# HGRN level scores with a stationary tile cut to the keys that a level uses

## The chip, the cores and the metric

The kernel runs on one core of one Trainium2 chip. The metric is the device time of one execution in microseconds. A profile of one execution, with the start and duration of every instruction on every engine, stands beside the times.

## What is computed

One hybrid decoder layer on 512 tokens of width 1024, in float32: a half-step SwiGLU network, a token mixer, and a second half-step SwiGLU network, each between RMS norms and added to its input. The mixer has four HGRN2 heads and four mLSTM heads, all causal. The change touches the scores of HGRN2:

```python
rel = G[:, :, :, None, :] - G[:, :, None, :, :]       # G: running sum of log forget gates
decay = jnp.exp(jnp.where(causal, rel, -jnp.inf))
scores = jnp.sum(qc[:, :, :, None, :] * kc[:, :, None, :, :] * decay, axis=-1)
o = o_inter + jnp.einsum("bhts,bhsv->bhtv", scores, vc)
```

The decay between a query and a key differs for each of the 128 channels, so that a score is no plain product of q and k.

## The kernel before

**The whole.** Three parts follow one another: the first SwiGLU network, the mixer, the second SwiGLU network. Almost all of TensorE's time goes into their large matrix products, done in split precision: every weight tile is split into a high part (ScalarE, line 273) and a low part (VectorE, line 275) of the format fp32r, and three products stand for one. The mixer's input projections are such products as well; lines 533 and 179 to 181 issue them. The small products of the mixer itself are plain float32.

**How HGRN scores are formed.** The sequence is handled in four chunks of 128 tokens, and the four heads as two pairs (`p` = 0 and 1), so that a pair has 8 blocks of 128 x 128 scores (2 heads x 4 chunks). Within such a block the diagonal is one product (`hgrn_diag`, line 1342). Everything below it is covered by seven levels, `LEVELS = (1, 64, 32, 16, 8, 4, 2)`. A level of size c cuts the 128 tokens into groups of 2c; queries are those in the second half of each group, keys those in the first half, and both are scaled by the decay to the group's middle, which makes the score a plain product. So each level has 64 queries and 64 keys of the 128 tokens. The queries are packed (64 columns, tile `qe`); the keys lie in their places in a tile of 128 columns (`ke`), whose other places hold older values. The product is thus 128 keys x 64 queries, and a mask (`mask`, one per level) picks the entries that count when they are copied to the score tile `sT` (line 1306). The last key that a level of size c uses is token 127 - c. Level 1 is different: one product with a column of ones (line 1298).

**Instructions of one level and pair.** VectorE and ScalarE prepare `qe` and `ke` (lines 1284 to 1291; the Exp of line 1287 writes the keys). TensorE then has 8 products (line 1302), one for each block of scores: the stationary tile is the keys (128 channels x 128 columns), the moving one the 64 queries, and all 8 go into one PSUM bank of 512 columns. VectorE copies under the mask.

**Order.** `hgrn_levels` steps through the levels of a pair by hand, each level being a generator that yields between its stages, so that the vector work of level n+1 is issued ahead of the product of level n. Between the steps `fill(per)` issues pieces of the mixer's input projections (`FILL` gives 6 pieces for the first pair, 5 for the second), which are filler work for TensorE. The two `ke` tiles alternate between levels, so the Exp of level n+2 waits for the product of level n. Each engine works through its own instructions in order. `job_rows` (line 1387) has a stationary tile of 100 columns, and the mLSTM scores (line 1476) use 64 of the 128 rows of the array.

Of the kernel before, what the change touches and what calls it, by code (L numbers as in the profile page):

```python
# [14 lines left out]
P = 128  # L15
# [100 lines left out]
class Layer:  # L116
# [179 lines left out]
    def flat(self, v):  # L296
        return v.rearrange("p a b -> p (a b)")
# [962 lines left out]
    def hgrn_edges(self, p, d):  # L1260
# [4 lines left out]
        for a in range(2):  # L1265
# [2 lines left out]
                nc.tensor.transpose(pt[:, c * P : (c + 1) * P], d[:, a, c * P : (c + 1) * P], self.ident)  # L1268
            nc.scalar.copy(self.kdt[:, 2 * p + a, :], pt[:, : 3 * P])

    def hgrn_level(self, p, n, ke):

        nc = self.nc
        c = LEVELS[n]
        q, kk, G = self.q[p], self.kk[p], self.G[p]
        flat = lambda t: t.rearrange("p a t -> p (a t)")
        blk = lambda t: flat(t).rearrange("p (b two c) -> p b two c", two=2, c=c)
        qe = self.st("qe")
        qe3 = qe.rearrange("p (b c) -> p b c", c=c)
        if c > 1:  # L1280
            el = self.st("el")
            el3 = el.rearrange("p (b c) -> p b c", c=c)
            ref = blk(G)[:, :, 0, c - 1 : c].broadcast_to([P, 512 // c, c])
            nc.vector.tensor_tensor(qe3, blk(G)[:, :, 1, :], ref, op=ALU.subtract)
            nc.vector.tensor_tensor(el3, ref, blk(kk)[:, :, 0, :], op=ALU.subtract)
            nc.scalar.activation(qe, qe, AF.Exp)
            nc.scalar.activation(blk(ke)[:, :, 0, :], el3, AF.Exp)
        else:
            nc.vector.tensor_scalar(qe3, blk(kk)[:, :, 1, :], -1.0, 1.0, op0=ALU.mult, op1=ALU.add)
        yield  # L1290
        nc.vector.tensor_tensor(qe3, qe3, blk(q)[:, :, 1, :], op=ALU.mult)
        if c == 1:

            nc.vector.tensor_tensor(qe3, qe3, blk(kk)[:, :, 0, :], op=ALU.mult)
        yield
        sc = self.ps()
        if c == 1:
            nc.tensor.matmul(sc, self.one.broadcast_to([P, P]), qe, start=True, stop=True)
        else:
            k8, q8 = flat(ke).rearrange("p (n s) -> p n s", s=P), qe.rearrange("p (n u) -> p n u", u=64)  # L1300
            for m in range(8):
                nc.tensor.matmul(sc[:, 64 * m : 64 * m + 64], k8[:, m], q8[:, m], start=True, stop=True)  # L1302
        yield
        so = self.sT[:, 8 * p : 8 * p + 8, :].rearrange("p n (b two c) -> p n b two c", two=2, c=c)[:, :, :, 1, :]
        mk = self.mask[:, n : n + 1, :].broadcast_to([P, 8, 64]).rearrange("p n (b c) -> p n b c", c=c)
        nc.vector.copy_predicated(so, mk, sc.rearrange("p (n b c) -> p n b c", n=8, c=c))
        yield

    def hgrn_levels(self, p, kes, per, then=lambda: None):
# [502 lines left out]
```

## Time and profile before

| | |
|---|---|
| median of 3 runs | 940.24 us (940.08 to 941.1) |
| profiled execution: span from first to last instruction | 938.5 us |
| TensorE clock granted over the span | 0.999 |
| busy share of the span: TensorE, VectorE, ScalarE, GpSimdE | 99%, 82%, 55%, 11% |
| passes of line 1302 | 192, started between 403.3 and 482.7 us |

In the profile's rows PE is TensorE's matmul, PEld its weight load (which runs beside matmuls), DVE is VectorE, ACT ScalarE, POOL GpSimdE; "q" behind an engine is its sequencer. L1302 is line 1302. A row of a group gives line, engine, operation, written and read tiles, shapes and the count; the stationary tile of a matmul stands as rows * columns ahead of the moving tile. Matmuls overlap in the pipeline, and their ends are modelled, so the distance between starts says more than a duration.

### The profile page before, as it was taken

How to read it: one execution, taken by the hardware profiler on the slowest of the kernel's cores; microseconds unless marked ns; L12 is line 12 of the kernel's file. 1: busy time of each engine (PE TensorE's matmuls, PEld its weight loads, DVE VectorE, ACT ScalarE, POOL GpSimd, SP SyncE). 2: the span in 40 equal slices, each digit the busy share in tenths (PEclk: the TensorE clock that was granted, in tenths of full speed). 3: DMA queues.
4: the chain of work that ended last, by engine and by line, in shares of the span. 5: the costliest groups of instructions: out<-in, count | busy, mean ns of one | idle time of the engine just before them, and what ended most of it. 6: DMA issues, size and time to landing. Idle time of an engine off the chain costs nothing.

```text
span 938.5 us, 18056 instructions
## 1 busy us (share of the span) xinstructions
PE 930.2 (99%) x7471; PEld 895.9 (95%) x7471; DVE 772.4 (82%) x1044; ACT 511.9 (55%) x735; POOL 107.4 (11%) x172
## 2 busy tenths in 40 slices
PE   9999999999999999999999999999999999999997
PEld 7999999999999999998887888899999999999997
DVE  6899988889988876698846564799899989998884
ACT  7645555557456467956622444495454545655541
POOL 3530000000001045200001210314000000000101
PEclk9999999999999999999999999999999999999999
DMA  9252433332352024321312124352354434323212
GB/s 319 87 157 91 126 123 113 93 111 72 118 170 90 24 84 124 111 68 45 91 45 68 45 76 139 123 173 65 124 158 135 135 115 156 113 87 121 87 45 90
DMA packets 86956, 101.35 MB, mean 108 GB/s; under 512 B 4277, under 2 KB 66777, under 8 KB 86874
## 3 DMA queue, kind: packets, MB, share of 16 engines
q1 hardware_dynamic: 86586, 99.68, 34.0%
q8 instruction: 58, 0.95, 0.4%
q10 hardware_dynamic: 288, 0.52, 0.2%
q14 instruction: 24, 0.20, 0.1%
HBM read 98.10 MB, written 2.10 MB: 107 GB/s over the span
## 4 chain that ended last, share of the span: by engine, by line
PE 63%; ACT 1%; issue 0%; DVE 0%; DVEq 0%; POOLq 0%; POOL 0%; ACTq 0%
PE ps L603 22%; PE ps L893 7%; PE ps L533 6%; PE ps L901 5%; PE ps L179 5%; PE ps L181 5%; PE ps L180 5%; PE ps L1302 2%; PE ps L543 1%; PE ps L348 1%; PE ps L1476 0%; PE ps L1387 0%; PE ps L1583 0%; PE ps L1556 0%; PE ps L1342 0%; PE ps L1580 0%
## 5 line engine op out<-in xcount | busy, mean ns | idle before, releaser
L273 ACT CAST w<-raw 128x1024 fp32r<-128x1024 f32 (+1 forms) x238 | 244.6, 1035 | 230.3 <-PE ps L603 93.5
L275 DVE TENSOR_TENSOR w<-raw,w 128x1024 fp32r<-128x1024 f32 (+1 forms) x238 | 290.9, 1228 | 36.3 <-ACT w L273 35.8
L603 PE MATMUL ps<-xq,w 128*128 128x256 f32 x2016 | 237.1, 277 | 0.0
L603 PEld LDWEIGHTS ps<-xq,w 128*128 128x128 f32 x2016 | 232.9, 188 | 0.0
L603 PE MATMUL ps<-sq,w 128*128 128x256 f32 x1512 | 177.9, 276 | 0.3
L603 PEld LDWEIGHTS ps<-sq,w 128*128 128x128 f32 x1512 | 174.3, 188 | 0.9 <-ACT ps L654 0.9
L893 PE MATMUL ps<-w,hs 128*128 128x256 f32 x960 | 113.0, 276 | 0.0
L893 PEld LDWEIGHTS ps<-w,hs 128*128 128x128 f32 x960 | 110.7, 188 | 0.0
L289 DVE TENSOR_TENSOR raw<-raw,raw 128x1024 f32<-128x1024 f32 x72 | 89.8, 1251 | 6.1 <-DMA raw<-in_ffn_w_in_dram 4.5
L179 PE MATMUL ps<-w,xq 128*128 128x512 f32 x192 | 78.7, 411 | 0.1
L180 PE MATMUL ps<-w,xq 128*128 128x512 f32 x192 | 74.9, 391 | 0.0
L181 PE MATMUL ps<-w,xq 128*128 128x512 f32 x192 | 74.9, 392 | 0.0
L438 POOL TENSOR_SCALAR col<-col 128x1 f32<-128x1 f32 x24 | 8.9, 372 | 513.7 <-ACT junk L437 513.7
L901 PE MATMUL ps<-w,hs 128*128 128x256 f32 x480 | 57.7, 276 | 0.0
L533 PE MATMUL ps<-xq,w 128*128 128x256 f32 x480 | 56.4, 278 | 0.0
L901 PEld LDWEIGHTS ps<-w,hs 128*128 128x128 f32 x480 | 55.9, 188 | 0.0
L533 PEld LDWEIGHTS ps<-xq,w 128*128 128x128 f32 x480 | 55.2, 188 | 0.5 <-issue 0.5
L179 PEld LDWEIGHTS ps<-w,xq 128*128 128x128 f32 x192 | 36.1, 188 | 8.3 <-issue 0.9
L181 PEld LDWEIGHTS ps<-w,xq 128*128 128x128 f32 x192 | 36.0, 188 | 8.1 <-DVE xq L355 0.3
L812 ACT CAST hs<-hf 128x1024 fp32r<-128x1024 f32 x32 | 33.6, 1052 | 17.6 <-PE ps L901 10.8
L180 PEld LDWEIGHTS ps<-w,xq 128*128 128x128 f32 x192 | 36.2, 188 | 7.0 <-DVE w L281 0.3
L813 DVE TENSOR_TENSOR hs<-hf,hs 128x1024 fp32r<-128x1024 f32 x32 | 39.0, 1219 | 1.3 <-ACT hs L812 1.2
(258 smaller groups left out, 1147.5 us busy)
## 6 DMA issues: line engine op xcount, KB each, us to landing
raw<-in_ffn_w_in_dram SPq DMA_DIRECT2D x98, 512.0 KB, 3.6
raw<-in_ffn_w_out_dram SPq DMA_DIRECT2D x44, 512.0 KB, 3.9
raw<-in_w_mix_in_dram SPq DMA_DIRECT2D x28, 512.0 KB, 3.6
raw<-in_w_mix_out_dram SPq DMA_DIRECT2D x8, 512.0 KB, 3.8
out_dram<-xs SPq DMA_DIRECT2D x8, 256.0 KB, 2.0
xs<-in_x_dram SPq DMA_DIRECT2D x6, 256.0 KB, 4.2
gpost<-in_norm_post_dram SPq DMA_DIRECT2D x3, 512.0 KB, 3.6
gpre<-in_norm_pre_dram SPq DMA_DIRECT2D x2, 512.0 KB, 3.8
```

What stands on the lines that cost most here:

```text
L179: mm(ps, sh, mh, start=start, stop=False, **kw)
L180: mm(ps, sh, ml, start=False, stop=False, **kw)
L181: mm(ps, sl, mh, start=False, stop=stop, **kw)
L273: nc.scalar.copy(hi, raw)
L275: self.low = nc.vector.tensor_tensor(lo, raw, hi.bitcast(F32), op=ALU.subtract)
L289: (nc.vector if late else nc.gpsimd).tensor_tensor(o, o, c, op=ALU.add)
L533: mm(ps[:, u0:u1], w[:, a, k, :], self.xop(k, b, u0, u1), start=k + n + m == 0, stop=k == ND - 1 and n == 2, skip_group_check=True,)
L603: self.nc.tensor.matmul(ps[:, c], wb[b][:, k, v], left[d][:, k, :], start=first and a + n + k == 0, stop=n == 2 and k == KH - 1, skip_grou ...
L812: self.nc.scalar.copy(hi, src)
L813: self.nc.vector.tensor_tensor(lo, src, hi.bitcast(F32), op=ALU.subtract)
L893: mm(out, a[kk][:, i * P : (i + 1) * P], w[:, b, kk, QUARTER * v : QUARTER * (v + 1)], start=begin and c == kk == n == 0, stop=kk == 1 and ...
L901: mm(ps[:, QUARTER * c : QUARTER * (c + 1)], A[a][:, c], B[b], start=begin and c == n == 0, stop=n == 2, skip_group_check=True,)
```

## The change

The stationary tile of a level's 8 products is cut to the first r columns: r = 128 - c, but not less than 72. That is 72, 96, 112, 120, 124 and 126 columns for the levels 64, 32, 16, 8, 4 and 2. The product then writes only the first r partitions of the bank, and the masked copy reads and writes only these. The entries left out are those that every mask had left out. Level 1 keeps 128. Lines behind the new function move down (1302 becomes 1307, 1306 becomes 1312).

```diff
+    def rows(self, c):
+
+        return P if c == 1 else max(P - c, 72)
+
     def hgrn_level(self, p, n, ke):
...
             k8, q8 = flat(ke).rearrange("p (n s) -> p n s", s=P), qe.rearrange("p (n u) -> p n u", u=64)
+            r = self.rows(c)
             for m in range(8):
-                nc.tensor.matmul(sc[:, 64 * m : 64 * m + 64], k8[:, m], q8[:, m], start=True, stop=True)
+                nc.tensor.matmul(sc[:r, 64 * m : 64 * m + 64], k8[:, m, :r], q8[:, m], start=True, stop=True)
         yield
+        r = self.rows(c)
         so = self.sT[:, 8 * p : 8 * p + 8, :].rearrange("p n (b two c) -> p n b two c", two=2, c=c)[:, :, :, 1, :]
         mk = self.mask[:, n : n + 1, :].broadcast_to([P, 8, 64]).rearrange("p n (b c) -> p n b c", c=c)
-        nc.vector.copy_predicated(so, mk, sc.rearrange("p (n b c) -> p n b c", n=8, c=c))
+        nc.vector.copy_predicated(so[:r], mk[:r], sc.rearrange("p (n b c) -> p n b c", n=8, c=c)[:r])
```

## The prediction

> **What bounds the kernel now.** I read the engine rows of the page first, then its chain, then the chain of waits between 400 and 490 us, where all edited instructions lie, and the windows and TensorE's waits behind that stretch.
>
> ```profile
> span 938.5 us, 18056 instructions
> PE 930.2 (99%) x7471; PEld 895.9 (95%) x7471; DVE 772.4 (82%) x1044; ACT 511.9 (55%) x735; POOL 107.4 (11%) x172
> PE 63%; ACT 1%; issue 0%; DVE 0%; DVEq 0%; POOLq 0%; POOL 0%; ACTq 0%
> ```
>
> The row of engines alone does not settle it, because matmul ends are modelled; but nearly everything else on the chain has a share of 0 or 1% and TensorE has 63%. TensorE is an in-order stream of matmul passes from end to end. Now the stretch itself, as columns busy time (count) for each engine, and, in the second fence, the longest waits in front of weight loads from 400 us on (total us, times, longest):
>
> ```profile
> 400.00:490.00 90.00, 90.00 (x595) 81.10 (x594) 68.59 (x100) 45.53 (x62) 1.40 (x1) 1.00 0.22 65
> 490.00:600.00 110.00, 109.86 (x557) 90.54 (x557) 66.00 (x147) 46.89 (x88) 20.19 (x38) 1.00 0.31 96
> 600.00:930.00 330.00, 329.72 (x2874) 328.11 (x2874) 296.86 (x363) 180.50 (x253) 22.38 (x32) 1.00 0.35 111
> ```
>
> ```profile
> PEld ps L603 <- ACT ps L654: 0.9, 3, 0.3
> PEld ps L179 <- issue: 0.9, 3, 0.4
> PEld ps L179 <- ACT xq L354: 0.7, 2, 0.4
> ```
>
> TensorE has no hole between 400 and 490 us (90.00 of 90.00), VectorE works 68.59 of it, the granted clock is 1.00. Behind the stretch no wait in front of a weight load adds up to more than 0.9 us. So time taken out of TensorE's stream between 400 and 490 us should come off the end of the kernel, unless an input comes late.
>
> The edited passes are line 1302 (weight load and matmul), listed with shortest, median and longest duration in ns, and the first and last start:
>
> ```profile
> L1302 PEld LDWEIGHTS ps<-qe,ke x192: 187/192/193, 403.3 to 482.7; 128*128 128x128 f32 x192
> L1302 PE MATMUL ps<-qe,ke x192: 217/275/275, 403.4 to 482.7; 128*128 128x64 f32 x192
> ```
>
> 96 matmul calls (2 head pairs x 6 levels x 8) make 192 passes, so a plain-fp32 matmul is two passes, each with its own weight load, in 12 blocks of 16. Durations overlap; what costs time is the pitch, from one start to the next. For that, one block in the order of time (start, length):
>
> ```profile
> 434.50 0.39 PE L181 MATMUL ps<-w,xq 128*128 128x512 f32 x1
> 434.73 1.89 PE L1302 MATMUL ps<-qe,ke 128*128 128x64 f32 x16
> 436.43 0.48 PE L179 MATMUL ps<-w,xq 128*128 128x512 f32 x1
> 436.75 0.39 PE L180 MATMUL ps<-w,xq 128*128 128x512 f32 x1
> 436.97 0.40 PE L181 MATMUL ps<-w,xq 128*128 128x512 f32 x1
> ```
>
> From the start at 434.50 to that at 436.75 are 2.25 us; the two filler passes L181 and L179 have 0.23 us each (434.50 to 434.73, and 436.75 to 436.97), which leaves 1.79 us for 16 passes: **112 ns a pass**, 21.5 us for all 192.
>
> **What paces the 112 ns.** Three candidates: streaming of the moving columns, issue, weight load.
>
> ```profile
> 441.50 1.78 PE ps L1342 x16
> 456.16 0.20 PE L1431 MATMUL ps<-ident,z 4*128 4x4 f32 x1
> 456.22 0.20 PE L1430 MATMUL ps<-ident,z 4*128 4x4 f32 x1
> 456.28 0.20 PE L1431 MATMUL ps<-ident,z 4*128 4x4 f32 x1
> ```
>
> Line 1342 (the diagonal) is also plain fp32, with 128 moving columns instead of 64, and its 16 passes take 1.78 us, 111 ns each. Twice the moving columns, the same pitch: streaming is not it. The tiny transposes start 0.06 us apart: issue allows at least that pitch. What line 1302 and line 1342 share is a stationary tile of 128 columns. The only narrower tile in this kernel is that of line 1387 (100 columns):
>
> ```profile
> L533 PEld LDWEIGHTS ps<-xq,w 128*128 128x128 f32 x267 | 31.1, 188 | 0.5 <-issue 0.5
> L1387 PEld LDWEIGHTS ps<-xq,gw 128*100 128x100 f32 x32 | 3.8, 164 | 0.0
> ```
>
> Its load takes 164 ns against 188: 24 ns less for 28 columns, **0.86 ns a column**. Only line 1387's duration is shown shorter, not its pitch, since its 256 moving columns hide the load.
>
> **The change, part by part.** The widths become 72, 96, 112, 120, 124 and 126 for the levels 64, 32, 16, 8, 4 and 2; that removes 56, 32, 16, 8, 4 and 2 columns, 118 in all, from each round of passes. At 0.86 ns the levels gain 48, 27, 14, 7, 3 and 2 ns a pass, together 101 ns; times 16 passes is 1.62 us, times two head pairs **3.24 us**. The narrowest pass would have a pitch of 112 - 48 = 64 ns, just above the 0.06 us of the transposes, so issue takes nothing back. Lower end of the gain: 0, if the pitch is no load's. Upper end: the pitch shrinks in proportion to the columns, 112/128 = 0.875 ns each: 118 x 0.875 x 32 = 3.30 us. I take 3.24, the measured slope.
>
> The Trainium skill, TensorE: Matmul & The Clock Gate, section LDWEIGHTS, gives a load as columns divided by 1.2, in ns; by it the sum would be an estimated 118 / 1.2 x 32 = 3.15 us. The slope in the rows above agrees within 3%.
>
> The other edits cost nothing either way. The masked copy of line 1306 gets 72 to 126 partitions instead of 128 but the same 512 elements in each; in the built programs order, counts and waits of the instructions are the same on every engine. If a narrower masked copy did change its time, VectorE's free time in the stretch (90 less 68.59 us) would cover 14 instructions.
>
> **Does the gain arrive?** The block with the least slack is the first of the second head pair; its keys come from this Exp (start, length), and it starts at the second row:
>
> ```profile
> 451.57 0.62 ACT L1287 ACTIVATE ke<-el 128x512 f32<-128x512 f32 x1
> 453.75 1.73 PE ps L1302 x16
> ```
>
> The Exp ends at 452.19 and the chain enters the block at 453.75 (its first pass starts some 0.16 us before): about 1.4 us of slack. TensorE comes there 1.62 us earlier. If ScalarE and VectorE did not move at all, TensorE would wait 0.2 us. But they do move in part: their work before it starts from TensorE's results, as in
>
> ```profile
> 409.91 1.05 ACT L273 CAST w<-raw 128x1024 fp32r<-128x1024 f32 x1 [0.73 <-PE ps L533]
> 432.18 1.05 ACT L273 CAST w<-raw 128x1024 fp32r<-128x1024 f32 x1 [2.58 <-PE ps L181]
> ```
>
> so I put this wait at 0, with 0.2 us for the range.
>
> From 616 us the chain runs in pieces of 68 us and more:
>
> ```profile
> 616.63 68.30 PE ps L603 x600
> 684.95 0.58 ACT ps L654
> ```
>
> VectorE is close behind there (296.86 of 330 us), but all its inputs come after the mixer, and its buffers come free as TensorE uses them up, so it shifts along. The three 0.58 us pieces of line 654 stay.
>
> **Rivals.**
>
> *The pitch is not the load's.* A fixed cost of a plain-fp32 pass at about 111 ns would fit lines 1302 and 1342 too. Then nothing moves: 940.2 us. For it: no row shows a full fp32 pass under 111 ns. Against it: the shorter load of line 1387, and the 0.06 us of the transposes. Chance 0.08.
>
> *The gain is partly taken back.* A late input (a weight split, or a score bank that is not yet copied out) makes TensorE wait behind several blocks. It would leave half or so: 938.6 us. Against it: no such wait stands there now, and the block behind the tightest one already has its keys (the Exp's end) 5.1 us ahead, as the others have them by several us:
>
> ```profile
> 454.63 0.63 ACT L1287 ACTIVATE ke<-el 128x512 f32<-128x512 f32 x1
> 460.36 1.73 PE ps L1302 x16
> ```
>
> Chance 0.08.
>
> *Another array setting.* If a tile under 128 columns makes TensorE change its setting at entry and exit of a block, the block pays for it. The kernel shows such a price where the 64-row score matmuls of mLSTM (line 1476) stand between fillers:
>
> ```profile
> 499.33 0.39 PE L181 MATMUL ps<-w,xq 128*128 128x512 f32 x1
> 499.65 1.16 PE L1476 MATMUL ps<-qk 64*128 64x128 f32 x8
> 500.74 0.50 PE L179 MATMUL ps<-w,xq 128*128 128x512 f32 x1
> 501.08 0.39 PE L180 MATMUL ps<-w,xq 128*128 128x512 f32 x1
> ```
>
> From 499.33 to 501.08 are 1.75 us; less two fillers of 0.23 and 8 passes of 0.112 leaves 0.39 us for one block. Twelve blocks cost 4.7 us, against a gain of 3.24: 1.4 us slower, 941.7 us. It decides from 0.27 us a block, and is over the resolution from 0.43 us. Against it stands line 1387 with its 100 columns, entered and left without such a hole:
>
> ```profile
> 417.86 1.43 PE ps L533 x12
> 419.29 3.76 PE ps L1387 x32
> 423.05 1.73 PE ps L1302 x16
> ```
>
> The pieces join without a gap, and 3.76/32 = 118 ns is hardly more than the 119 of the 128-column fillers before it (1.43/12). Chance 0.06, half of it over the resolution. The Trainium skill, TensorEngine Tiling (Array Packing), section Key Properties, says that a change of the tiling mode drains TensorE, and its section When to Use Tiling places column tiling at 64 columns and less. By that rule 72 columns stay clear of it; no run here shows 64.
>
> *Load and stream stop overlapping for a narrow tile.* Then a pass costs load plus stream: at 72 columns 64 + 56 = 120 ns (an estimate: half of line 1342's 111 ns for streaming 64 columns). With 56 ns more and 0.86 ns a removed column less on each level the 12 blocks cost (6 x 56 - 101) x 32 = 7.5 us more: 947.7 us. Line 1387 speaks against it, whose pitch of 118 ns leaves no room for load and 256 columns one after the other. Chance 0.03.
>
> **The numbers.** The profiled execution's span is 938.5 us; the median of the runs is 940.24, 1.8 us above, for what lies around the span. The forecast is span 935.3 and time 940.24 - 3.24 = **937.0 us**, chance 0.75. The range is 936.3 (3.30 us gained, and the scatter of the three runs, 940.08 to 941.1, on the low side with some for the edges of the blocks) to 939.2 (a third of the gain left); it leaves out the first, third and fourth rivals, 17 in 100. A measurement of this kernel can tell about 0.2%, 1.9 us, from no change. Faster by more than that: the forecast and half of the partial case, 0.79. Within: half of the partial case, the first rival, half of the third: 0.15. Slower: the rest, 0.06.
>
> **What would show it.** In the changed profile, line 1307's blocks should take 16 x 64, 85, 98, 105, 109 and 110 ns from filler to filler; the level of 64 alone falls from 1.79 to about 1.02 us. Weight loads of 72 columns should last about 144 ns instead of 192. If loads get shorter and pitches do not, the first rival is right; if filler passes around the blocks stretch as around line 1476, the third; if pitches shrink and the span does not, waits in front of weight loads will name what came late. I am wrong if the blocks stay at 1.79 us.

## The result and the profile after

| | before | changed |
|---|---|---|
| median of 7 runs each | 940.9 us (940.08 to 941.46) | 937.52 us (936.86 to 939.23) |
| ratio, with its 95% interval | | 0.9972 (0.9961 to 0.9982) |
| profiled execution: span | 938.5 us | 937.5 us |

The kernel is faster by 0.28%, 2.6 us (1.7 to 3.7), the medians differ by 3.4. The profiled execution of the changed kernel was the longest of the seven (939.23 us), so its span shows only 1.0 us; where the rest went is told below.

The row of engines and the chain by engine:

```profile
span 937.5 us, 18056 instructions
PE 929.0 (99%) x7471; PEld 894.4 (95%) x7471; DVE 772.9 (82%) x1044; ACT 511.5 (55%) x735; POOL 107.1 (11%) x172
```

Nothing has changed in kind: the same number of instructions, TensorE busy all the time. The chain of waits, cut to the twelve edited blocks (start, length):

```profile
404.49 1.03 PE ps L1307 x16
...
410.42 1.33 PE ps L1307 x16
...
416.04 1.53 PE ps L1307 x16
...
422.76 1.63 PE ps L1307 x16
...
428.58 1.68 PE ps L1307 x16
...
434.46 1.71 PE ps L1307 x16
...
453.30 1.03 PE ps L1307 x16
...
459.20 1.33 PE ps L1307 x16
```

Every block stood at 1.73 us before. Now the lengths follow the widths 72, 96, 112, 120, 124 and 126, and the second head pair repeats the first. The twelve add up to 17.8 us against 20.8: **2.9 us out of TensorE's stream**. The weight loads of 400 to 485 us, by shape (total us, mean ns):

```profile
L1307 PEld LDWEIGHTS ps<-qe,ke 128*126 128x126 f32 x32 | 3.8, 190 | 0.2
L1307 PEld LDWEIGHTS ps<-qe,ke 128*112 128x112 f32 x32 | 3.4, 178 | 0.1
L1307 PEld LDWEIGHTS ps<-qe,ke 128*96 128x96 f32 x32 | 3.0, 165 | 0.1
L1307 PEld LDWEIGHTS ps<-qe,ke 128*72 128x72 f32 x32 | 2.4, 145 | 0.1
```

From 126 to 72 columns a load gets 45 ns shorter, 0.83 ns a column. From the second pass of a block on, the starts lie 64.9, 85.0, 98.1, 104.9, 108.2 and 110.0 ns apart for the six widths, against 111.6 before: again 0.83 ns a column, so that pitch and load shrink together. The recorded load lasts some 80 ns longer than the pitch at either end (145 against 64.9, 192 against 111.6), so loads overlap, and only their slope carries over to the pitch.

The edges of a block, in the order of time, level 2 of the first pair:

```profile
434.06 0.40 PE L181 MATMUL ps<-w,xq 128*128 128x512 f32 x1
434.30 1.87 PE L1307 MATMUL ps<-qe,ke 128*126 128x64 f32 x16
435.98 0.48 PE L179 MATMUL ps<-w,xq 128*128 128x512 f32 x1
436.29 0.39 PE L180 MATMUL ps<-w,xq 128*128 128x512 f32 x1
```

434.06 to 436.29 is 2.23 us; less two fillers of 0.23 and 16 x 0.110 leaves 0.01. A tile of 126 columns has no price at its edges; 72 columns are shown between fillers below. The longest waits in front of weight loads from 400 us on are the ones of before:

```profile
PEld ps L179 <- issue: 0.9, 3, 0.4
PEld ps L603 <- ACT ps L654: 0.9, 3, 0.3
PEld ps L179 <- ACT xq L354: 0.7, 2, 0.4
```

**Why the span shows less.** Up to 340 us this execution was 0.8 us ahead, from its start. Then it lost 1.7 us before the first edited instruction. The groups of TensorE's matmuls from 356 to 386 us, first of the kernel before, then of the changed one:

```profile
L533 PE MATMUL ps<-xq,w 128*128 128x256 f32 x267 | 30.4, 276 | 0.0
```

```profile
L533 PE MATMUL ps<-xq,w 128*128 128x256 f32 x257 | 30.4, 281 | 0.0
```

The same code issues 257 passes instead of 267 in these 30 us: each takes 281 instead of 276 ns, and the pitch is 118 instead of 113. In the changed kernel's execution this lasted from 347 to 389 us (337 passes, 1.6 us) and again from 774 to 793 us (162 passes, 0.8 us). Runs of the kernel before scatter by about as much: of 24 on one chip 16 lay at 939.6 to 940.6 us and 8 at 941.1 to 942.5. Whether such stretches part the two groups is not shown; the one profile of that kernel has no long one.

### The profile page after: what moved, and what is told of

Its sections match the earlier page's. It is cut to its first block, busy times and chain, and to the rows that moved or that the text cites. A ratio compares the mean times of both kernels' runs of the same rounds, so it can differ in the third digit from the quotient of the medians.

```text
span 937.5 us, 18056 instructions
## 1 busy us (share of the span) xinstructions
PE 929.0 (99%) x7471; PEld 894.4 (95%) x7471; DVE 772.9 (82%) x1044; ACT 511.5 (55%) x735; POOL 107.1 (11%) x172
## 4 chain that ended last, share of the span: by engine, by line
PE 61%; ACT 1%; DMA 0%; DVE 0%; issue 0%; POOL 0%; DVEq 0%; POOLq 0%; ACTq 0%; SPq 0%
PE ps L603 22%; PE ps L893 7%; PE ps L533 6%; PE ps L901 5%; PE ps L179 5%; PE ps L181 4%; PE ps L180 4%; PE ps L1307 2%; PE ps L348 1%; PE ps L543 1%; PE ps L1482 0%; DMA raw<-in_ffn_w_in_dram 0%; PE ps L1393 0%; PE ps L1589 0%; PE ps L1562 0%; PE ps L1348 0%
## 5 line engine op out<-in xcount | busy, mean ns | idle before, releaser
L901 PEld LDWEIGHTS ps<-w,hs 128*128 128x128 f32 x480 | 55.9, 188 | 0.0
```

Source lines behind the costliest of these rows:

```text
L901: mm(ps[:, QUARTER * c : QUARTER * (c + 1)], A[a][:, c], B[b], start=begin and c == n == 0, stop=n == 2, skip_group_check=True,)
```

## The experiments

Theory: the weight load paces a plain-fp32 pass with 64 moving columns, a load costs 0.83 ns a column, and TensorE's time between 400 and 490 us arrives whole. Rivals: late inputs take part of it back; a narrow tile costs at the edges of its block; VectorE's narrower copy has a share; the long stretches at 118 ns belong to the change.

### The changed kernel again

No edit.

> The changed kernel once more, to part what the change does from what one execution does. Theory: the level blocks take 1.03, 1.30, 1.50, 1.60, 1.65 and 1.68 us again, to 0.03 us, and the time is 2.6 to 3.4 us under that of the kernel before. In the profiled execution of the changed kernel 256-column passes ran at a pitch of 118 instead of 113 ns from 346.9 to 388.8 us, ahead of the first edited instruction, and from 773.7 to 793.2 us. If these stretches belong to the execution and not to the kernel, they lie elsewhere or have other lengths here. Rival: the change brings them (through what it does to the order of events); then they stand at the same places, and with them some 2.5 us of extra time.

Measured: 938.48 us (937.36 to 939.37, 6 runs) against 940.4, ratio 0.9972 (0.9961 to 0.9984): 2.6 us (1.5 to 3.7) by the ratio, at the low end of what was expected, and 1.9 by the medians, below it. The blocks are the same to 0.01 us. The profiled execution (span 935.6 us) has the short pitch in the window from 356 to 386 us:

```profile
L533 PE MATMUL ps<-xq,w 128*128 128x256 f32 x267 | 30.4, 276 | 0.0
```

The stretch at 118 ns ended at 353 us here, and the second one (774 to 793 us) is not there at all. So these stretches belong to the execution. Added up over all 256-column passes at the long pitch, the time above 113 ns a pass is 5.0 us in the first profile of the changed kernel and 2.4 in this one, some 2.5 us less; the spans show 1.9 of it (937.5 against 935.6), and other places give 0.6 back.

### Level 64 alone

```diff
-        return P if c == 1 else max(P - c, 72)
+        return 72 if c == 64 else P
```

> Only level 64 is narrowed (72 columns), the five other levels keep 128. Theory (the weight load paces the pass, and TensorE's time arrives whole): its two blocks fall from 1.73 to 1.03 us, the other ten stay at 1.70, and the time falls by 1.4 us. Rival (a narrow tile costs a change of setting at the block's edges, 0.39 us a block): the passes beside the two blocks stretch, and the time falls by 0.6 us.

Measured: 938.85 us (12 runs) against 940.4, ratio 0.9981 (0.9972 to 0.999), 1.8 us (0.9 to 2.6). From the chain of waits, the first three blocks and the first of the second pair:

```profile
403.25 1.03 PE ps L1307 x16
...
409.05 1.73 PE ps L1307 x16
...
415.08 1.73 PE ps L1307 x16
...
452.71 1.03 PE ps L1307 x16
```

Two blocks of 1.03, ten of 1.73: 1.4 us, as the theory has it, inside the interval; 0.6 us is outside. Level 64 alone brings half of the change.

### All levels with 72 columns

```diff
-        return P if c == 1 else max(P - c, 72)
+        return P if c == 1 else 72
```

> All six levels use 72 columns, so that scores of keys beyond the 72nd are left out. Theory: all twelve blocks fall to 1.03 us, 8.2 us together, and the time falls by 8.2 us if every input is still in time. Rival (the gain is partly taken back by late inputs): TensorE then comes to the first block of the second head pair some 4 us earlier, against a slack of 1.4 us; if ScalarE and VectorE do not move along at all, it waits 2.7 us there and the time falls by 5.5 us; a wait in front of line 1307's weight load shows it.

Measured: 931.61 us (5 runs) against 940.4, ratio 0.9907 (0.9894 to 0.9921): 8.7 us (7.4 to 10.0). All twelve blocks stand at 1.03 in the chain, 8.4 us together. At the block with the least slack, the Exp of its keys and the block:

```profile
447.31 0.61 ACT L1291 ACTIVATE ke<-el 128x512 f32<-128x512 f32 x1
```

```profile
448.44 0.39 PE L181 MATMUL ps<-w,xq 128*128 128x512 f32 x1
448.67 1.19 PE L1307 MATMUL ps<-qe,ke 128*72 128x64 f32 x16
```

The block starts 4.9 us earlier than before the change (448.67 against 453.59), the Exp 4.3 us earlier (447.31 against 451.57): ScalarE moved along; its casts wait for TensorE's results, as the rows in the prediction show. The slack fell from 1.4 to 0.75 us and the filler is followed by the block at its usual 0.23 us. No wait for a late input appears here; the rival's 5.5 us is outside the interval.

The next block stands between fillers; the filler ahead of it and the second one behind it:

```profile
454.34 0.39 PE L181 MATMUL ps<-w,xq 128*128 128x512 f32 x1
...
455.89 0.40 PE L180 MATMUL ps<-w,xq 128*128 128x512 f32 x1
```

That is 1.55 us, where a block with 128 columns has 2.25: 0.70 us less, 15 times the 46.7 ns between the pitches. So 72 columns have no price at the edges either.

### The narrower copy alone

```diff
-                nc.tensor.matmul(sc[:r, 64 * m : 64 * m + 64], k8[:, m, :r], q8[:, m], start=True, stop=True)
+                nc.tensor.matmul(sc[:, 64 * m : 64 * m + 64], k8[:, m], q8[:, m], start=True, stop=True)
```

> Only the masked copy is narrowed to 72 to 126 partitions; the products keep 128 columns. Theory: the copies keep their 0.73 us, the blocks their 1.70, and the time does not move (within 0.5 us). Rival (part of the gain is VectorE's): the copies get shorter with the partitions and the time falls.

Measured: 941.5 us (11 runs) against 940.4, ratio 1.0005 (0.9996 to 1.0014). The copies of all seven levels (shortest, median, longest in ns):

```profile
L1312 DVE COPY_PREDICATED sT<-mask,ps x14: 714/734/1330, 394.2 to 484.2; 128x512 f32<-128x512 int32 x2, 72x512 f32<-72x512 int32 x2, 96x512 f32<-96x512 int32 x2, 112x512 f32<-112x512 int32 x2
```

Level by level the copies last what they lasted with 128 partitions, to 0.02 us: 0.71 to 0.74 us for the levels 64 to 4, and 1.30 to 1.33 for the levels 1 and 2 in both kernels. Fewer partitions do not shorten a copy of the same 512 elements. The gain is all TensorE's. The profile of this kernel, whose products are those of before, has a 118 ns stretch from 347 to 389 us too, so the narrower products are not needed for one.

### Level 64 with 64 columns

```diff
-        return P if c == 1 else max(P - c, 72)
+        return P if c == 1 else P - c
```

> The changed kernel, but level 64 gets the 64 columns that it uses instead of 72. Theory (the load alone paces): 8 columns less give a pitch of 58 ns, or the 62 ns of the tiny transposes if issue stops it there; the two blocks fall from 1.03 to 0.93 or 0.99 us, and the time by 0.1 to 0.2 us against the changed kernel, too little to be measured. Rival (64 columns are another setting of the array, with a price at both edges of a block as at line 1476): each of the two blocks costs some 0.4 us more, seen at the passes beside them, and the time rises by 0.6 us against the changed kernel.

Measured: 939.21 us (8 runs) against 941.68, ratio 0.9975 (0.9964 to 0.9985); the changed kernel has 0.9972 on other chips, and the two can't be told apart by these times. The trace can tell. The order of time around the first block of the second pair:

```profile
453.49 0.39 PE L181 MATMUL ps<-w,xq 128*128 128x512 f32 x1
453.80 1.15 PE L1307 MATMUL ps<-qe,ke 128*64 128x64 f32 x16
454.88 0.87 PE L1268 MATMUL ps<-ident,ek 128*128 128x128 f32 x6
455.68 0.22 PE L1436 MATMUL ps<-ident,z 4*128 4x4 f32 x1
```

The filler is followed by the block after 0.31 us instead of 0.23. Inside the block the pitch is 58.3 ns, less than at 72 columns, but the block takes 1.08 us instead of 1.03. From the filler to the small transposes are 2.19 us, against 2.01 in the changed kernel (452.91 to 454.92). So the rival has its point: at 64 columns there is a price. Against the changed kernel it is 0.18 us a block, not the 0.4 expected, because the shorter pitch gives 0.10 us of it back (15 x 6.6 ns).

### One width for each level

```diff
-        return P if c == 1 else max(P - c, 72)
+        return {1: P, 64: 68, 32: 65, 16: 64, 8: 48, 4: 33, 2: 32}[c]
```

> One width for each level, to read the pitch of a pass as a function of the columns: 68, 65, 64, 48, 33 and 32 columns for the levels 64, 32, 16, 8, 4 and 2; scores of the keys beyond are left out. Theory (load of 0.83 ns a column and 5 ns): 62, 59, 58, 45, 33 and 32 ns, or a floor of about 56 to 62 ns where streaming or issue takes over. Rival (settings of 64 and 32 columns have a price): blocks of 64 columns and fewer get longer at their edges by some 0.4 us, those of 65 and 68 do not.

Measured: 933.44 us (2 runs) against 941.68, ratio 0.9912 (0.9894 to 0.993). From the chain, the first pair:

```profile
402.89 0.98 PE ps L1307 x16
...
408.63 0.94 PE ps L1307 x16
...
413.73 1.07 PE ps L1307 x16
...
420.14 1.02 PE ps L1307 x16
...
425.50 1.01 PE ps L1307 x16
...
430.84 1.01 PE ps L1307 x16
```

68 and 65 columns go on down, 0.98 and 0.94; 64 is longer, 1.07, and 48 to 32 stay at 1.01 to 1.02. Inside the blocks the pitch is 61.6, 59.1, 58.3, 55.9, 55.8 and 55.8 ns: the load's 0.83 ns a column down to 64, and then a floor at 56 ns. Streaming is the likely reason: plain-fp32 passes with 258 moving columns (line 1535 of the kernel before) start 217 ns apart, 0.84 ns a column, which makes an estimated 54 ns for 64. No run changed the moving columns, so this is not shown. The price at the edges, where fillers stand on both sides (64 columns, second pair):

```profile
459.04 0.40 PE L181 MATMUL ps<-w,xq 128*128 128x512 f32 x1
459.37 1.15 PE L1307 MATMUL ps<-qe,ke 128*64 128x64 f32 x16
460.44 0.50 PE L179 MATMUL ps<-w,xq 128*128 128x512 f32 x1
460.78 0.40 PE L180 MATMUL ps<-w,xq 128*128 128x512 f32 x1
```

1.74 us less two fillers of 0.23 and 16 x 0.058 leaves 0.35 us for one block, close to the 0.39 of line 1476. The same two fillers around the block of 65 columns just before:

```profile
454.60 0.39 PE L181 MATMUL ps<-w,xq 128*128 128x512 f32 x1
...
456.06 0.39 PE L180 MATMUL ps<-w,xq 128*128 128x512 f32 x1
```

That is 1.46 us, 0.28 less than with 64 columns. By the sum above, 65 columns would leave 0.05 us as well, since one step of the sixteen does not follow the pitch; so 0.28 to 0.30 us is what the step from 65 to 64 columns costs a block between fillers. The step lies between 64 and 65 columns.

### Level 64 with 65 columns, beside the changed kernel

```diff
-        return P if c == 1 else max(P - c, 72)
+        return P if c == 1 else max(P - c, 65)
```

> The changed kernel with 65 instead of 72 columns for level 64, the narrowest tile that ran at 59 ns a pass without a price at its edges when the widths were varied by level. Theory: its two blocks take 0.91 to 0.94 us instead of 1.03, the time is 0.2 us under that of the changed kernel and 2.8 to 3.4 us under that of the kernel before; the 0.2 us can be seen in the blocks, not in the times. Rival (any tile near 64 columns costs at its edges): the passes beside the blocks stretch as they did with 64 columns, by 0.05 to 0.09 us each.

> The changed kernel a third time, on the chip of the run with 65 columns, for the comparison and for a third look at the long stretches with a pitch of 118 ns. Theory: 2.6 to 3.4 us under the kernel before; a stretch from about 347 to 389 us is there in one execution and not in another, worth 1.5 us. Rival: the stretch is a property of the kernel, then it is here if and only if it was in both earlier profiles of the changed kernel.

Measured, on one chip, against 940.11 us (11 runs): 65 columns 937.32 us (5 runs), ratio 0.9965 (0.9952 to 0.9979); the changed kernel 937.45 us (7 runs), ratio 0.9972 (0.9961 to 0.9983). With 65 columns, the same place as above:

```profile
451.95 0.39 PE L181 MATMUL ps<-w,xq 128*128 128x512 f32 x1
452.18 1.10 PE L1307 MATMUL ps<-qe,ke 128*65 128x64 f32 x16
453.12 0.82 PE L1268 MATMUL ps<-ident,ek 128*128 128x128 f32 x6
453.88 0.22 PE L1436 MATMUL ps<-ident,z 4*128 4x4 f32 x1
```

1.93 us from filler to transposes, 0.26 less than with 64 columns. The block takes 0.94 us instead of the 1.03 at 72 columns, at both places: 0.18 us in all. It is the least work for TensorE of the versions that compute everything; the times can't show a step of that size. The third profile of the changed kernel has no stretch at 118 ns from 347 to 389 us, but one from 773 to 792: each of its three profiles is different in this.

## Why the prediction was right

- **The place of the gain.** TensorE's stream is the kernel's time, and it shrank where it was said to. No longer wait took the place of the 2.9 us, and with all levels at 72 columns not even of 8.4 us. From the start of the first edited pass to the end of the span, the profile before has 535.0 us, the second one of the changed kernel 532.6 and that with 72 columns everywhere 527.0: 2.4 and 8.0 us less. The missing 0.4 to 0.5 us lie behind the blocks; the kernel with the narrower copy alone is 0.2 us longer there too, so part of it may be scatter, but its source is open.
- **What paces the pass.** Shown: the pitch follows the columns of the stationary tile from 128 to 64, with 64 moving columns throughout. The first rival (a fixed cost of an fp32 pass near 111 ns) is out. So is the fourth: at 72 columns a pass takes 65 ns, not 120.
- **The slope.** Taken as 0.86 ns a column from one row of 100 columns; measured 0.83. That this came so near is in part luck: the row of 164 ns was set against the 188 of line 533, and against the edited line's own 192 it would have given 1.0 ns a column and 3.8 us. Line 1302's loads last 4 ns longer than line 533's at the same width, a difference between lines that the prediction did not separate from the width. The Trainium skill's load of columns divided by 1.2 (TensorE: Matmul & The Clock Gate, section LDWEIGHTS) is 0.83 ns a column: here the Trainium skill was nearer than my row, and the pitches inside the blocks agree with its slope. The recorded loads agree in slope alone: 72 columns last 145 ns, where by the Trainium skill's rule it would be an estimated 60. The forecast of 144 ns for a load of 72 columns stands against 145 measured.
- **The sum.** 3.24 us was forecast, 2.9 measured in the stream. Two terms were too large: the slope, by 3%, and the count. I let all 16 passes of a block gain, but only 15 of the steps from start to start do. The first step of a block stayed at 55 to 61 ns, before and after; the step out of it shrank with the width (84 ns before, 57 at 96 columns). The pitches shrank by 98.5 ns in all on the six levels; x 15 x 2 that is about 2.95 us. The measured 937.52 us lies nearer to the forecast of 937.0 than these terms deserve: the medians differ by 3.4 us, the ratio gives 2.6, and the median before moved from 940.24 with three runs to 940.9 with seven. That part of the agreement is luck.
- **The slack.** Put at 1.4 us for the tightest block, with the wait at 0 because ScalarE moves along. In the run with 72 columns everywhere it moved 4.3 of 4.9 us. The step was right, and the 0.2 us kept for it were not needed. (The 5.1 us for the block behind it was counted to the chain's row; to the first pass, 0.16 us ahead, it is 4.9.)
- **The third rival.** A price exists, somewhat under the one feared (0.28 to 0.35 us against 0.39, by how it is counted), but it begins at 64 columns, not below 128. The bound of 72 in the change keeps clear of it. The rule of the Trainium skill (TensorEngine Tiling (Array Packing), section When to Use Tiling: column tiling from 64 columns down; section Key Properties: a drain when the mode changes) agrees with the step between 64 and 65; that a drain is what these 0.28 to 0.35 us are was not shown.
- **What was missed.** The scatter between executions. The range's reach below and above came from three runs that spread over 1 us; two profiles of the changed kernel, one with and one without the long stretches at 118 ns, lie 1.9 us apart, against the 2.9 that the change takes out of the stream.

## What to carry to other kernels

When TensorE is the bound and a matmul has few moving columns, look at the pitch from start to start rather than at busy times: if it stays the same for twice the moving columns, streaming does not set it, and a narrower stationary tile shows whether the weight load does. Here each stationary column that isn't needed was worth 0.83 ns a pass, down to a floor of 56 ns for 64 moving columns of plain fp32. Stop above 64 columns if the neighbours use the whole array: one column less cost 0.26 to 0.28 us a block here. For effects of a few tenths of a per cent add up the edited rows of the trace, and take several profiles of each kernel before reading one span against another.

## What the runs showed of the hardware that was not expected

The same 256-column passes run at one of two pitches, 113 or 118 ns (durations 276 and 281), in stretches that can last 40 us, at a granted clock of 1.00 in either. The stretches begin behind short interruptions of the stream (behind the transposes at 342 to 349 us, for one) and in some executions persist up to 389 us where they end at 353 us in others. Of three profiles of the changed kernel one has this long stretch; the kernel with the narrower copy alone and that with 64 columns have it too, and the one profile of the kernel before does not. What decides between the two was not tried and stays open.

A masked copy in VectorE takes the same time with 72 as with 128 partitions (0.73 us for the 512 elements of level 64), and a tile of 65 columns is loaded and streamed without any price at its edges while 64 has one.
